# Loading the first x columns and the first weight in halves, and moving three small steps and one weight load in the state-space layer of a two-layer trunk

## The chip, the cores and the metric

The kernel runs on one core of a Trainium2 chip. The metric is the device time of one execution in microseconds (us); the time of a kernel is the median of several runs. One run of each kernel was also recorded by the hardware profiler, and the rows in this document come from that recording. Engines are named as in the profile: PE does the matrix products and the transposes, PEld its weight loads, DVE is the vector engine, ACT the scalar engine, POOL the GpSimd engine, SP the engine that issues most DMAs. Each engine runs its instructions in order; what follows an instruction that waits, waits too.

## The reference

The input x is 1024 frames by 1024 channels in float32. Two layers run one after the other, each adding to x. Cut to what matters:

```python
# layer 0: state-space mixer
h = rmsnorm(x, norm_g[0])
branch, gate = split(h @ s5_w_in[0])            # 1024 x 2048 weight
y = gelu(s5_mixer(branch, ...))                 # 64 groups, 16 channels -> 64 complex states
y = y * sigmoid(y @ s5_w_glu[0] + s5_b_glu[0])
x = x + (y * silu(gate)) @ s5_w_out[0]
# layer 1: gMLP mixer
u, v, gate = split(rmsnorm(x, norm_g[1]) @ sgu_w_in[0])
x = x + (sgu_mixer(gelu(u), gelu(v), ...) * silu(gate)) @ sgu_w_out[0]
return rmsnorm(x, final_g)
```

## The kernel before

Every float32 matrix product is done as three products of "hi" and "lo" parts: hi is the value rounded to the format that PE reads, lo the rest. For the input projection x is transposed by PE (`x_turn`), ACT copies the rounded part into `ahi` (`x_hi`), and DVE writes the difference into `alo` (`x_lo`). A weight panel of 128 columns is loaded into a raw buffer by SP (`w_load`), ACT rounds it into `w_hi` and DVE or POOL subtracts into `w_lo` (`w_split`). There is one raw buffer until a second one is added late; w_load of the next panel waits until the subtraction has read the buffer.

The input projection has 16 output tiles i, each in two halves of 512 frames; a half is 8 steps k of three matmuls with 512 columns. `in_mm` issues the steps and `in_out` (called `evict` later) has DVE multiply the finished PSUM bank by the row factors into the tile `stage`, from where `in_store` writes it to memory. Until all of layer 0's units are done the bank of a half is chosen by a counter modulo the number of banks in the list `banks["mm"]`: four at the beginning, two during the units, four again afterwards. A half can start only when the half that had its bank before is evicted.

At the start the four row blocks of x come in four loads of 512 columns, then weight 0 in one load. PE turns four column blocks, ACT and DVE split them, the weight is split by ACT and POOL, and DVE does some scalar preparation in between (`pull(n)` runs n small instructions of it). While the first three output tiles are computed, the preparation ends, `make_b0(0)` builds the first batch of a small table (three POOL instructions, the tile printed as `b`, from `br`, `bi`, `bn`, `bs`), `phases()` builds the phase table `ph` on POOL, and `tab_ops(0)` builds the first rotation table `e` on POOL.

Then come 19 periods, p from -3 to 15, one for each of 16 units of four groups. A period interleaves, on every engine in the written order, the work of units p, p+1, p+2, p+3 and some steps of the input projection: `mm(n)` takes the next n steps from the list `todo`; when it has taken the last step of a half it appends the half to the list `outs`; `evict()` takes the first entry of `outs`, and does nothing when the list is empty. `FILL0` gives one step at each of the five places of a period with p below 0, `FILL` gives 2, 2, 2, 2, 1 afterwards. `outs` starts with (2, 1) and (3, 0), `todo` with (3, 1), (4, 0), (4, 1) and so on. In period p unit p is rotated (`rot_co` on DVE, `rot_si` on POOL, `rot_add` on DVE, with the table `cs` that SP copies from `e`), scanned (`scan`, the tile `gg`), and rotated back. The first `evict()` of a period stands behind `rot_add` and `scan` on DVE. `k_mm(p+2)` on PE reads the table `b`; batch 1 is built by `make_b0(1)` at the end of period -2.

Unit outputs go to memory (`y_d`) and come back as tiles `lo` through `load_y(k)`: eight DMAs for each k, on SP, the odd ones of k = 7 on ACT. `y_split(k)` splits them on ACT and DVE. Behind period 15 all of load_y(4) to load_y(7) is issued, and then a loop over k takes five steps of the projection, one eviction, one `y_split` and, when a whole tile of the projection is done, a `split` of the weight two tiles on and a `queue` that loads the one after. The last such weight, number 16, is the first panel of the next product (`w_glu`, 384 matmuls).

Up to here `in_order[0]` is true and the order on each engine is the written one. Behind it a planner orders the instructions.

Of the kernel before, what the change touches and what calls it, by code (L numbers as in the profile page):

```python
# [19 lines left out]
F32R = mybir.dt.float32r  # L20
# [6 lines left out]
P = 128  # L27
# [33 lines left out]
def trunk(ctx, tc, x, norm_g, final_g, s5_w_in, A_re, A_im, log_dt, B_re, B_im, C_re, C_im,  # L61
# [211 lines left out]
    def x_hi(half, k):  # L273
        S.activation(ahi[:, k, half * HALF:(half + 1) * HALF], x_ps[half, k], AF.Copy, scale=g0[:, k:k + 1])
# [44 lines left out]

    def in_mm(i, half, ks, between=lambda: None):  # L320
        if ks[0] == 0:
            in_ps[i, half] = mmps()
        hi, lo = in_w[i]
        cs = slice(half * HALF, (half + 1) * HALF)
        ps = in_ps[i, half]
        for k in ks:
            T.matmul(ps, lhsT=hi[:, k], rhs=ahi[:, k, cs], start=k == 0, stop=False)
            T.matmul(ps, lhsT=hi[:, k], rhs=alo[:, k, cs], start=False, stop=False)
        between()
        for k in ks:  # L330
            T.matmul(ps, lhsT=lo[:, k], rhs=ahi[:, k, cs], start=False, stop=k == KT - 1)
# [406 lines left out]
    Q.dma_start(g0, norm_g[0].rearrange("(k p) -> p k", p=P))  # L738
    for b in range(4):
        load_x(0, b, b + 1, 0, HALF)  # L740
    w_load(0)
    load_x(0, 0, 2, HALF, D)
# [44 lines left out]

    for k in range(4):
        x_turn(0, k)
        x_hi(0, k)  # L790
        if k == 2:
            pull(4)
        x_lo(0, k)
        if k == 1:
            w_split(0, GP)
    pull(13)
    in_mm(0, 0, range(0, 4), lambda: x_turns(0, range(4, 8)))
    for k in range(4, 8):
        x_hi(0, k)
        x_lo(0, k)  # L800
    in_mm(0, 0, range(4, 8))
    w_load(2)
# [49 lines left out]
    pull(99)  # L852
    make_b0(0)
    phases()
    c_turn(1)
# [52 lines left out]
    def period(p):  # L908
# [13 lines left out]
        if p == 0:  # L922
            for _ in gen:
                pass
        if here:
            swap_in(p)
            rot_co(p)
            rot_si(p)
# [44 lines left out]
        if p % 2 == 0 and 2 <= p + 4 < 16:  # L973
            put_powers((p + 4) // 2)
            make_b0((p + 4) // 2)

# [8 lines left out]
    for p, ks in ((14, (0,)), (15, (1, 2, 3))):  # L985
        for k in ks:
            load_y(k)
        period(p)
    for k in range(4, 7):
        load_y(k)  # L990
    for i in range(UG):
        out_mm(15, i)
    out_copy(15)
    load_y(7)
    wk_cm.__exit__(None, None, None)
# [5 lines left out]
    for k in range(KT):  # L1001
        mm(5)
        evict()
        y_split(k)
        split(V)
        queue()
# [244 lines left out]
```

## Time and profile before

| | |
|---|---|
| runs, us | 856.35, 854.26, 852.93 |
| median, us | 854.26 |
| profiled execution, us | 857.32 |
| its span, us | 855.2 |
| mean granted clock of PE in it | 0.985 |
| PE busy | 96% of the span |
| DVE, ACT, POOL busy | 60%, 34%, 27% |

The span is from the first to the last instruction of the program; 2.1 us of the profiled execution lie around it. A busy share is an average over stages. In the views, a timeline row is start, length, engine, operation, tiles written and read, shapes, count, and in brackets the engine's idle time before it and what ended that. The clock column of a windows row is the share of full speed that PE was granted: 1.00 is 2.4 GHz, 0.50 is 1.2 GHz.

### The profile page before, as it was taken

Reading aid. Unit: us, or ns where it says so; the run is one execution under the profiler, and the core shown is the slowest. Engines: PE = TensorE matmul, PEld = TensorE weight load, DVE = VectorE, ACT = ScalarE, POOL = GpSimd, SP = SyncE. Lnnn points to the kernel's source line nnn. Section 1 sums busy time; section 2 is a strip of 40 time slices with the busy share of each in tenths; the row PEclk is TensorE's granted clock in tenths of the full one; section 3 lists DMA queues with packets and bytes.
Section 4 is the critical chain, followed back from the end, with each engine's and each line's share of the span. In section 5 each row is a group of like instructions: output and inputs, shape, how many; then the busy total and the mean of one; then the engine's idle time right before and its main releaser. Section 6 shows DMA issues by size and latency. Waiting matters only on the chain.

```text
span 855.2 us, 10992 instructions
## 1 busy us (share of the span) xinstructions
PE 822.1 (96%) x3962; PEld 669.5 (78%) x3962; DVE 511.9 (60%) x1097; ACT 293.8 (34%) x519; POOL 228.9 (27%) x261
## 2 busy tenths in 40 slices
PE   7998899999998999989999999999999899999996
PEld 6776687888886888868888888888888688888884
DVE  8888888888635977863277211211599945452255
ACT  4632444444433765453122322211412122332122
POOL 2059877787520000000000000000057512113221
PEclk9999999999999999989999999999999899999998
DMA  9727787888988623464012321300400012380022
GB/s 278 109 72 185 178 226 197 203 211 203 239 191 190 212 69 111 147 221 125 25 74 82 122 68 49 101 23 1 147 1 1 25 50 77 103 256 9 1 99 98
DMA packets 122678, 102.25 MB, mean 120 GB/s; under 512 B 20480, under 2 KB 103424, under 8 KB 122624
## 3 DMA queue, kind: packets, MB, share of 16 engines
q1 hardware_dynamic: 112144, 94.93, 40.0%
q10 hardware_dynamic: 10480, 6.62, 2.5%
q8 instruction: 31, 0.51, 0.2%
q14 instruction: 23, 0.19, 0.1%
HBM read 67.45 MB, written 25.17 MB: 108 GB/s over the span
## 4 chain that ended last, share of the span: by engine, by line
PE 57%; DVE 18%; DMA 10%; POOL 5%; ACT 4%; issue 3%; SPq 2%; DVEq 0%; POOLq 0%; ACTq 0%
PE mm L74 52%; PE aux L74 5%; DVE c L74 5%; DVE lo L74 4%; DMA lo<-y_d 2%; DMA raw<-in_s_w_in 2%; SPq L74 2%; ACT c L74 2%; POOL w_lo L74 1%; DVE w_lo L74 1%; DMA raw<-in_s_w_out 1%; DVE t L74 1%; POOL e L74 1%; DMA raw<-in_sgu_w_in 1%; POOL et L74 1%
## 5 line engine op out<-in xcount | busy, mean ns | idle before, releaser
L74 PE MATMUL mm<-ahi,w_hi 128*128 128x512 f32 x512 | 210.2, 411 | 3.8 <-DVE stage L74 3.3
L74 PE MATMUL mm<-alo,w_hi 128*128 128x512 f32 x512 | 202.2, 395 | 1.8 <-DVE alo L74 1.8
L74 PE MATMUL mm<-ahi,w_lo 128*128 128x512 f32 x512 | 196.3, 396 | 0.0
L74 PEld LDWEIGHTS mm<-ahi,w_hi 128*128 128x128 f32 x512 | 97.2, 190 | 24.9 <-DVE stage L74 4.1
L74 PEld LDWEIGHTS mm<-alo,w_hi 128*128 128x128 f32 x512 | 97.4, 190 | 21.5 <-DVE alo L74 3.3
L74 PEld LDWEIGHTS mm<-ahi,w_lo 128*128 128x128 f32 x512 | 97.0, 190 | 21.6
L74 DVE TENSOR_TENSOR w_lo<-raw,w_hi 128x1024 fp32r<-128x1024 f32 x28 | 40.4, 1442 | 69.5 <-ACT w_hi L74 69.5
L74 PE MATMUL mm<-c,ahi 128*128 128x512 f32 x256 | 80.3, 396 | 0.0
L74 POOL TENSOR_TENSOR lo<-lo,lnb 128x128 f32<-128x128 f32 x64 | 34.5, 568 | 162.0 <-DVE lo L74 162.0
L74 ACT ACTIVATE w_hi<-raw 128x1024 fp32r<-128x1024 f32 x38 | 40.1, 1056 | 70.0 <-PE mm L74 50.9
L74 POOL TENSOR_SCALAR_AFFINE_SELECT wsn<-wsn 128x1024 f32<-128x1024 f32 x1 | 1.1, 1092 | 231.2 <-DMA wsn<-in_sgu_w_s 231.2
L74 DVE TENSOR_TENSOR c<-mm,c 128x512 f32<-128x512 f32 x32 | 21.9, 691 | 65.3 <-PE mm L74 65.3
L74 PEld LDWEIGHTS mm<-c,ahi 128*128 128x128 f32 x256 | 48.1, 188 | 11.7
L74 PE MATMUL mm<-hi,ahi 128*128 128x512 f32 x128 | 52.0, 407 | 3.0 <-ACT hi L74 2.9
L74 PE MATMUL mm<-hi,w_hi 128*128 128x512 f32 x128 | 51.2, 400 | 2.6 <-ACT w_hi L74 2.6
L74 DVE TENSOR_TENSOR c<-c 128x512 f32<-128x512 f32 x64 | 50.1, 835 | 3.2 <-POOL c L74 3.1
L74 PE MATMUL mm<-hi,alo 128*128 128x512 f32 x128 | 51.9, 407 | 0.0
L74 PE MATMUL mm<-lo,ahi 128*128 128x512 f32 x128 | 51.9, 405 | 0.0
L74 PE MATMUL mm<-lo,w_hi 128*128 128x512 f32 x128 | 51.3, 401 | 0.0
L74 PE MATMUL mm<-hi,w_lo 128*128 128x512 f32 x128 | 51.1, 401 | 0.0
L74 PE MATMUL mm<-ahi,hi 128*128 128x512 f32 x128 | 50.6, 396 | 0.0
L74 PE MATMUL mm<-alo,hi 128*128 128x512 f32 x128 | 50.6, 395 | 0.0
(173 smaller groups left out, 1483.1 us busy)
## 6 DMA issues: line engine op xcount, KB each, us to landing
raw<-in_sgu_w_in SPq DMA_DIRECT2D x24, 512.0 KB, 3.7
cs<-e SPq DMA_DIRECT2D x32, 256.0 KB, 3.9
raw<-in_s_w_in SPq DMA_DIRECT2D x14, 512.0 KB, 5.6
u_d<-stage SPq DMA_DIRECT2D x8, 512.0 KB, 5.3
us<-u_d SPq DMA_DIRECT2D x16, 256.0 KB, 5.1
t_d<-kpad SPq DMA_DIRECT2D x64, 64.0 KB, 3.0
traw<-t_d SPq DMA_DIRECT2D x16, 256.0 KB, 5.3
y_d<-ysb ACTq DMA_DIRECT2D x16, 256.0 KB, 3.2
```

The source lines that it names most:

```text
L74: ins = getattr(self.engine, name)(*args, **kwargs)
```

## The change

Five edits. First, x's first 512 rows come in two loads of 256 columns with half of weight 0 behind each; the weight is split half by half (`w0_split`), `in_mm0` issues the first output half in smaller pieces (the products of `w_lo` apart, so that `in_mm` loses its `between`), and the preparation instructions are pulled 4, 4 and 9 at a time where it was 4 and 13. Second, `make_b0(1)` is issued with `make_b0(0)` ahead of `phases()`, and no longer at the end of period -2. Third, period 0 calls `evict()` once more, ahead of unit 0's rotation. Fourth, behind unit 15 nine steps of the projection, one eviction, the split of weight 15 and the load of weight 16 come ahead of load_y(6) and load_y(7); until then only two banks are in the list. Fifth, the loop over k takes its last steps one turn earlier.

```diff
-    def in_mm(i, half, ks, between=lambda: None):
+    def in_mm(i, half, ks):
...
-        between()
...
-    for b in range(4):
-        load_x(0, b, b + 1, 0, HALF)
-    w_load(0)
+    in_raw[0] = raw_tile([P, KT, P])
+    for q in range(2):
+        load_x(0, 0, 4, q * 256, (q + 1) * 256)
+        Q.dma_start(in_raw[0][:, q * 4:(q + 1) * 4],
+                    s5_w_in[0][q * HALF:(q + 1) * HALF, 0:P].rearrange("(k p) c -> p k c", p=P))
...
-    for k in range(4):
-        x_turn(0, k)
-        x_hi(0, k)
-        if k == 2:
-            pull(4)
-        x_lo(0, k)
-        if k == 1:
-            w_split(0, GP)
-    pull(13)
-    in_mm(0, 0, range(0, 4), lambda: x_turns(0, range(4, 8)))
+    w0 = in_w[0] = [wsp.tile([P, KT, P], F32R, name=f"w_{c}", tag=c) for c in ("hi", "lo")]
+
+    def w0_split(q):
+        ks = slice(q * 4, (q + 1) * 4)
+        S.activation(w0[0][:, ks], in_raw[0][:, ks], AF.Copy)
+        sub_hi(GP, w0[1][:, ks], in_raw[0][:, ks], w0[0][:, ks])
+
+    def in_mm0(ks, part):
+
+        if (0, 0) not in in_ps:
+            in_ps[0, 0] = mmps()
+        for k in ks:
+            for j, src in ((0, ahi), (0, alo)) if part == 0 else ((1, ahi),):
+                T.matmul(in_ps[0, 0], lhsT=w0[j][:, k], rhs=src[:, k, 0:HALF], start=(k, part) == (0, 0) and src is ahi,
+                         stop=(k, part) == (KT - 1, 1))
+
+    for q in range(2):
+        for k in (2 * q, 2 * q + 1):
+            x_turn(0, k)
+            x_hi(0, k)
+            x_lo(0, k)
+        w0_split(q)
+        pull(4)
+        in_mm0((2 * q, 2 * q + 1), 0)
+    pull(9)
+    x_turns(0, range(4, 8))
+    in_mm0(range(0, 4), 1)
     for k in range(4, 8):
         x_hi(0, k)
         x_lo(0, k)
-    in_mm(0, 0, range(4, 8))
+        in_mm0((k,), 0)
+    in_mm0(range(4, 8), 1)
...
     make_b0(0)
+    make_b0(1)
     phases()
...
         if p == 0:
             for _ in gen:
                 pass
+            evict()
         if here:
             swap_in(p)
             rot_co(p)
...
             put_powers((p + 4) // 2)
-            make_b0((p + 4) // 2)
+            if p >= 0:
+                make_b0((p + 4) // 2)
...
-    for k in range(4, 7):
-        load_y(k)
+    load_y(4)
+    load_y(5)
     for i in range(UG):
         out_mm(15, i)
     out_copy(15)
+    mm(9)
+    evict()
+    split(V)
+    queue()
+    load_y(6)
     load_y(7)
...
     banks.update(mm=[0, 1, 2, 3], aux=[4, 5, 6, 7])
     for k in range(KT):
-        mm(5)
-        evict()
+        if k != KT - 1:
+            mm(5)
+            evict()
         y_split(k)
         split(V)
         queue()
```

## Rows read from the trace of the kernel before

**Rows 1.** The page, part 1: busy time, share of the span, number of instructions.

```profile
PE 822.1 (96%) x3962; PEld 669.5 (78%) x3962; DVE 511.9 (60%) x1097; ACT 293.8 (34%) x519; POOL 228.9 (27%) x261
```

**Rows 2.** Waits of PE: who was waited for, us in total, times, longest.

```profile
PE mm L74 <- DVE stage L74: 3.3, 2, 2.8
PE mm L74 <- ACT w_hi L74: 3.0, 2, 2.6
...
PE aux L74 <- POOL b L74: 1.3, 1, 1.3
```

**Rows 3.** Windows: length; busy of PE, PEld, DVE, ACT, POOL; clock, DMA share, GB/s.

```profile
12.05:14.25 2.20, 0.36 (x2) 0.00 (x0) 2.20 (x3) 0.04 (x1) 1.41 (x1) 1.00 1.14 338
...
92.00:95.40 3.40, 3.40 (x12) 2.71 (x11) 3.30 (x6) 1.76 (x3) 3.24 (x6) 0.50 0.45 74
272.80:275.45 2.65, 0.12 (x1) 0.00 (x0) 0.00 (x0) 1.07 (x2) 0.00 (x0) 1.00 1.10 385
276.20:279.60 3.40, 3.40 (x10) 2.38 (x9) 3.40 (x6) 3.24 (x6) 0.00 (x0) 0.52 1.11 357
371.90:378.80 6.90, 6.12 (x14) 4.24 (x15) 4.58 (x7) 4.86 (x8) 0.00 (x0) 0.51 0.66 224
```

**Rows 4.** Timeline of DVE, POOL, PE and ACT at the start, 9 to 20 us.

```profile
9.27 1.41 DVE L74 SCALAR_TENSOR_TENSOR alo<-aux,g,ahi 128x512 fp32r<-128x512 f32 x2
...
11.13 2.41 DVE L74 TENSOR_SCALAR t<-t 128x128 f32<-128x128 f32 x1
...
17.01 2.71 DVE L74 SCALAR_TENSOR_TENSOR alo<-aux,g,ahi 128x512 fp32r<-128x512 f32 x4
...
11.08 2.38 POOL L74 TENSOR_TENSOR w_lo<-raw,w_hi 128x1024 fp32r<-128x1024 f32 x1 [4.28 <-ACT w_hi L74]
...
15.25 1.91 PE L74 MATMUL aux<-ident,xh 128*128 128x128 f32 x16
...
15.89 2.42 ACT L74 ACTIVATE ahi<-aux,g 128x512 fp32r<-128x512 f32 x4 [3.80 <-PE aux L74]
```

**Rows 5.** Timeline: POOL's last of make_b0(0), DVE beside it, POOL's last of make_b0(1).

```profile
54.51 4.38 POOL L74 TENSOR_TENSOR b<-b,b0t 128x128 f32<-128x128 f32 x1
...
54.86 0.70 DVE L74 TENSOR_TENSOR mu<-lp,br 128x512 f32<-128x512 f32 x1
...
82.57 0.45 POOL L74 TENSOR_TENSOR b<-b,b0t 128x128 f32<-128x128 f32 x1
```

**Rows 6.** Timeline of SP and DVE around unit 0's rotation, 81 to 91 us.

```profile
81.80 3.14 SPq L74 DMA_DIRECT2D cs<-e  x4
...
86.34 0.70 DVE L74 TENSOR_TENSOR rot<-rot,cs 128x512 f32<-128x512 f32 x1 [2.60 <-DMA cs<-e]
...
89.75 1.05 DVE L74 TENSOR_TENSOR stage<-mm,rb 128x512 f32<-128x512 f32 x1
```

**Rows 7.** Timeline of DVE: the last eviction ahead of the one in rows 6.

```profile
74.76 1.13 DVE L74 TENSOR_TENSOR stage<-mm,rb 128x512 f32<-128x512 f32 x1
```

**Rows 8.** Timeline behind unit 15; last, the DMA view of a load issued at 72.93.

```profile
244.50 0.48 PE L74 MATMUL mm<-ahi,w_hi 128*128 128x512 f32 x1
...
250.33 0.39 SPq L74 DMA_DIRECT2D raw<-in_s_w_in  x1
...
251.40 18.01 SPq L74 DMA_DIRECT2D lo<-y_d  x28
269.45 0.43 SPq L74 DMA_DIRECT2D raw<-in_s_w_glu  x1
...
249.52 3.67 ACTq L74 DMA_DIRECT2D lo<-y_d  x4
...
256.23 1.06 ACT L74 ACTIVATE w_hi<-raw 128x1024 fp32r<-128x1024 f32 x1 [0.71 <-DMA raw<-in_s_w_in]
...
258.19 1.22 DVE L74 TENSOR_TENSOR w_lo<-raw,w_hi 128x1024 fp32r<-128x1024 f32 x1
...
raw<-in_s_w_in SPq DMA_DIRECT2D x1, 512.0 KB, 4.2
```

## The prediction, made before the changed kernel was run

> **What bounds the kernel now.** I read the page's busy shares first, then the list of what PE waited for, then windows with the granted clock around the longest of those waits, and last the timelines of the engines there. PE is busy for 822.1 us, 96% of the span [rows 1]. So an edit is worth what it takes from PE's idle time or adds to it. All edits act before 283 us. Behind that point 384 matmuls of the next product follow, and they need about 0.23 us each, so what PE gains or loses before is carried to the end. In the part touched, PE's longest waits are 2.8 us for an eviction (the tile stage), 2.6 us for the rounded weight 16 and 1.3 us for the table b [rows 2]. The reader should look at the clock too. After the wait for the weight (PE idle from 272.9 to 275.5) PE runs at 0.52 for 3.4 us, and after the wait for the eviction at 0.50 for 3.4 us: the level of 1.2 GHz instead of 2.4. That costs half of 3.4, 1.7 us, each time. At 12.05 PE stood nearly idle for 2.2 us and the clock stayed at 1.00 [rows 3].
>
> **The start.** The loads become finer, but x is not what comes last there. DVE can't split a column of x before 9.27, because its preparation runs until then, and two columns take it to 10.68. Later DVE stands in one small instruction for 2.41 us, because POOL subtracts the weight at the same time, for 2.38 us. The last four columns start at 17.01, and PE's last products of that half wait for them [rows 4]. So the question is whether DVE comes to 17.01 earlier. In the changed order PE issues the products of columns 0 and 1 first, and the last of these needs the split at 10.68; it is through at 11.0. Only then it turns columns 2 and 3. A column takes 0.5 us to turn (16 column pieces, four to a column, in 1.91 us) and 0.6 us to copy [rows 4], so DVE splits columns 2 and 3, 0.68 each (four in 2.71), from about 12.4 to 13.7. ACT copies the second half of the weight from 12.8 to 13.4, and POOL subtracts it for half of 2.38, 1.2 us, to about 14.7. DVE's 13 small instructions begin at 13.7, stand behind that to 14.7, and need 2.1 us more (in the trace the block ends at 13.5, two column splits take 1.4, and these instructions the rest to 17.0). That gives 16.8 in place of 17.0. The long block is split, but DVE's wait for PE's turns takes what it frees. I take -0.2 us, with bounds of -0.7 (the small instructions get in before POOL's second half) and +0.4 (x's pieces of 1 KB land later than its rows of 2 KB; PE's turn of the second pair then waits). The load of weight 2, which waits for POOL's subtraction, leaves SP 1.2 us later, and those of bn, weight 3 and bs queue behind it on SP. All of x's second half is split and multiplied before the first of their users, and that hides it; without this cover it would cost the 1.2.
>
> **Two batches of beta B ahead.** The three instructions of make_b0(1) end at 83.02 [rows 5], and SP starts to copy the table e at 81.80 [rows 6], when POOL has just finished it: the three cost POOL 1.2 us. Taking them from there removes PE's wait of 1.3 us for b. But they now stand ahead of phases() and of e, which POOL builds one behind the other, so e is done 1.2 us later. The chain goes on from e: SP's copies at 81.80; DVE's rotation at 86.34, which waits for them (2.60 us); then scan and eviction, which ends at 90.8 [rows 6] and lets PE go on. All of that comes 1.2 us later. PE saves 1.3 us on the way and then waits longer for the eviction. I take +1.2 us. PE is idle from about 86.5 to 92.1 then, 5.6 us in place of 2.8. Whether the half level afterwards lasts 3.4 us or 6.9, as at 371.9 [rows 3], I can't tell: bounds 0 (the new instructions find a gap on POOL) and +2.9.
>
> **One more eviction in period 0.** It does nothing. With one step at each of five places, periods -3 to -1 take 15 steps of todo: all eight of (3, 1) and seven of (4, 0). The evictions of (2, 1), (3, 0) and (3, 1) have been issued, the last at 74.76 [rows 7], and the next one in the trace is that at 89.75. The eighth step of (4, 0) is issued in the first mm of period 0, behind the new call. So outs is empty there, and the call returns. Cost 0, and the wait of 2.8 us stays.
>
> **Weight 16 ahead of the last y loads.** SP issues 28 pieces of y in 18.01 us and only then, at 269.45, the load of weight 16, for which PE waits [rows 8]. In the new order 12 of them come behind it, 12 x 0.64 = 7.7 us, so it leaves at about 262 and lands near 268 (5.8 us, as weight 15 took), before PE needs it. That takes away 2.6 us of waiting and the 1.7 us of the half level, 4.3 us. The last y pieces are late by one issue at most, and are needed only at the seventh and eighth step of the next product.
>
> What is late next is a bank. Nine steps now run while the list has two banks. The counter gives (13, 1) bank 1 (27 modulo 2) where it gave bank 3, and (14, 1), number 29, takes bank 1 of four. So (14, 1) waits for the eviction of (13, 1). On DVE that now stands behind the subtraction of weight 15, which stands behind ACT's rounding, which waits for the landing of weight 15. PE's 123 matmuls from 244.50 to 272.8 are 0.230 us apart, so it comes to (14, 1), 51 matmuls in, at 256.2. Weight 15 is issued at 250.33. In the trace it lands at about 256.1 (ACT starts at 256.23), 5.8 us later; a load of the same size on a quiet queue took 4.2 us [rows 8], that is 254.5. Four pieces of y that ACT issues at 249.52 are in its way now and will come behind it, so I take 255.2. From there on 0.1 + 1.06 for the rounding, 1.2 for the subtraction and 0.7 for the eviction with its hand-over: PE goes on 3.1 us after the landing, at 258.3. The new wait is 2.1 us (bounds 1.4 and 3.0; 0 if the weight lands far earlier than any such load did). The wait of 2.2 us at 12.05 left the clock alone, those of 2.6 and 2.8 did not; I take no half level here. Together -4.3 + 2.1 = -2.2 us, bounds -4.3 and +0.4 (3.0 with a half level).
>
> Sum: -0.2 + 1.2 + 0 - 2.2 = -1.2 us. The profiled execution took 857.32 us (span 855.2), so it would take 856.1. It lies 3.1 us above the median of the runs, 854.26; taken from that, 853.1 us.
>
> **The rivals.** (1) Weight 15 lands so early that (14, 1) hardly waits: -0.2 + 1.2 - 4.3 = -3.3, 851.0 us. For it speaks that the queue is freer; against it, that no such load took under 4.2 us. Chance 0.13. (2) The new wait takes 3.0 us and brings the half level again: -0.2 + 1.2 + 0.4 = +1.4, 855.7 us. That is today's landing unchanged. Chance 0.14. (3) POOL's new instructions cost the chain nothing. The last one of make_b0(0) took 4.38 us where its like takes 0.45, while DVE ran products of SBUF tiles of 0.70 us, one behind the other [rows 5]; if the new ones could slip into that run, phases() would begin as today, and the sum is -1.2 - 1.2 = -2.4, 851.9 us. The row speaks against it, since the first one didn't slip in. The Trainium skill (SBUF — State Buffer, Who interferes with whom) says that the two engines share a port pair, and that the one that comes second waits until the first one's instruction has ended; by that, POOL would get in after one DVE instruction of 0.7 us, which is the time of this rival. The row shows a wait through several such instructions, so I hold to the row. Chance 0.05. (4) The wait for the eviction at unit 0 goes away, as the call's place suggests: -0.2 - 1.3 - 2.8 - 1.7 - 2.2 = -8.2, 846.1 us. The count of steps excludes it unless the lists run otherwise than I read them. Chance 0.03. (5) Slower: ACT stands still at its four issues of y. They come behind the rounding of weight 15 now and ahead of every y_split, and took 3.67 us in the trace [rows 8], part of it waiting. If each waits for pieces of y that SP issues late, ACT's splits start late. DVE's chain behind them has 16 pieces of 0.68, a weight of 1.2 and an eviction, about 13 us, and PE wants the last piece at 272.8 + 2.1 + 21 x 0.23 = 279.7. So from 266.7 on each us that ACT stands longer costs PE one. If ACT stood until 272.7, about 3 us behind SP's last issue of y, that is 6.0: -1.2 + 6.0 = +4.8, 859.1 us. For it speaks that the issues have moved behind others; against it, that SP is still at the fifth tile of y when ACT comes to them. Chance 0.07.
>
> **How the numbers follow.** My forecast has 0.55. The rest, 0.03, is the planner, which orders everything behind the first layer's units and may order it otherwise. The measurement can tell about 0.5%, 4.3 us, from no change. The range takes in rivals 1 to 3: down to -0.7 + 1.2 - 4.3 = -3.8, 850.5 us, and up to +0.4 + 1.8 + 0.4 = +2.6, 856.9 us (1.8: the chain's 1.2 and a third of the longer half level's 1.7). Faster by more than 0.5% are rival 4 and the lower tails of the forecast, of rival 1 and of the planner, 0.12; slower by more, most of rival 5 and the upper tails of rival 2 (a longer half level) and of the planner, 0.11; the rest, 0.77, lies within.
>
> **What would show it.** In the changed kernel's profile: DVE's last four splits at the start still begin near 17; PE's wait for b is gone; SP's first copies of cs start 1.2 us later against DVE's preparation, and PE's wait for stage at unit 0 has grown to about 5 us; no eviction stands ahead of unit 0's rotation; a new wait for stage of about 2 us at 256; none for w_hi at 273. I am wrong if the start gains over 1 us, if PE doesn't wait at 256, or if an eviction appears ahead of the rotation.

## The result, and the profile of the changed kernel

| | before | changed |
|---|---|---|
| median, us (10 runs each) | 854.59 | 860.97 |
| lowest and highest, us | 852.57 to 857.16 | 856.81 to 862.11 |
| profiled execution, us (span) | 857.32 (855.2) | 862.11 (860.4) |

The ratio is 1.007, with a 95% interval of 1.0056 to 1.0083: the changed kernel is slower by 6.0 us (4.8 to 7.1). The prediction was 853.1 us with a range up to 856.9, so it was wrong, and in direction too. Of its three terms that aren't zero, one held in the profiles (+1.2 for beta B) and two fell (-0.2 for the start, -2.2 for the tail).

Busy time, the line that answers to [rows 1]: PE is busy 2.6 us longer for the same 3962 instructions; its mean granted clock was 0.979 where it was 0.985.

```profile
PE 824.7 (96%) x3962; PEld 670.7 (78%) x3962; DVE 511.7 (59%) x1097; ACT 293.7 (34%) x520; POOL 228.8 (27%) x262
```

Waits of PE (us in total, times, longest), against [rows 2]: the wait for b is gone, that for the tile stage has grown from 2.8 to 5.5, and a wait of 2.0 for lo, the split of y, is new. What is left for w_hi is a wait at the start.

```profile
PE mm L74 <- DVE stage L74: 6.6, 3, 5.5
...
PE mm L74 <- DVE lo L74: 2.0, 1, 2.0
...
PE mm L74 <- ACT w_hi L74: 1.3, 1, 1.3
```

Windows of the changed kernel (columns as in [rows 3]), each inside a stretch at a granted clock of 0.50: at the start (the stretch lasts from 8.5 to 15.4 us), behind unit 0's eviction (6.8 us, from 93.9 to 100.7, where it was 3.4), and behind the wait for lo (3.4 us, from 288.4 to 291.8).

```profile
9.50:15.30 5.80, 4.50 (x18) 3.61 (x17) 4.50 (x15) 2.09 (x4) 1.28 (x1) 0.50 1.09 354
94.00:100.30 6.30, 4.79 (x13) 3.88 (x14) 5.63 (x10) 3.72 (x8) 5.52 (x7) 0.50 0.34 63
288.60:291.00 2.40, 2.40 (x7) 1.92 (x6) 2.40 (x4) 2.40 (x4) 0.00 (x0) 0.50 0.41 164
```

At the start this column can't be compared with before. Before shows 1.00 there, but its trace has no record of the clock ahead of 10.1 us. Its first turns began 0.21 us apart up to 10.0 us, twice the 0.11 us of the 16 at 15.25 [rows 4]: the spacing of the lower level. So by the spacing that level ended at 10 us in before and at 15.4 in the changed kernel. The turns in before:

```profile
7.15 3.37 PE L74 MATMUL aux<-ident,xh 128*128 128x128 f32 x16
```

DVE at the start, against [rows 4]: it waits 3.46 us for log_dt and then is late by 1.7 us at the first split of x and by 3.4 at the last four (20.40 against 17.01). In between it waits 1.70 for the turns of columns 2 and 3.

```profile
5.47 0.66 DVE L74 TENSOR_SCALAR t<-t 128x64 f32<-128x64 f32 x3 [3.46 <-DMA t<-in_s_log_dt]
...
10.94 1.41 DVE L74 SCALAR_TENSOR_TENSOR alo<-aux,g,ahi 128x512 fp32r<-128x512 f32 x2
12.27 1.38 DVE L74 SCALAR_TENSOR_TENSOR t<-t,t 128x128 f32<-128x128 f32 x1
...
15.82 1.41 DVE L74 SCALAR_TENSOR_TENSOR alo<-aux,g,ahi 128x512 fp32r<-128x512 f32 x2 [1.70 <-ACT ahi L74]
...
20.40 2.71 DVE L74 SCALAR_TENSOR_TENSOR alo<-aux,g,ahi 128x512 fp32r<-128x512 f32 x4
```

That log_dt and A_im land late stands in the DMA view (queue, KB, and us from issue to landing). First the kernel before, then the changed one; both issue the three small loads at 0.81, 1.30 and 1.95 to 1.96.

```profile
t<-in_s_log_dt ACTq DMA_DIRECT2D x1, 32.0 KB, 3.3
...
t<-in_s_A_im ACTq DMA_DIRECT2D x1, 16.0 KB, 4.6
```

```profile
raw<-in_s_w_in SPq DMA_DIRECT2D x1, 256.0 KB, 6.1
t<-in_s_log_dt ACTq DMA_DIRECT2D x1, 32.0 KB, 4.6
...
t<-in_s_A_im ACTq DMA_DIRECT2D x1, 16.0 KB, 6.3
```

Around unit 0, against [rows 6]: DVE's rotation at 91.17, behind a wait of 4.15 us for cs, then the eviction, then PE. No eviction stands ahead of the rotation: the extra call did nothing.

```profile
91.17 0.70 DVE L74 TENSOR_TENSOR rot<-rot,cs 128x512 f32<-128x512 f32 x1 [4.15 <-DMA cs<-e]
...
94.40 1.05 DVE L74 TENSOR_TENSOR stage<-mm,rb 128x512 f32<-128x512 f32 x1
...
95.50 0.79 PE L74 MATMUL mm<-ahi,w_hi 128*128 128x512 f32 x1 [5.55 <-DVE stage L74]
```

In the tail, against [rows 8]: the wait for the bank at 262 is there, 0.76 us. Then come two stands of DVE that I had not foreseen: 4.05 us until the store of tile 13 has been done, and 1.80 us at a product of the next block (the tile c) that waits for its load. The eviction of (15,1) and the last two y splits stand behind that, and PE waits for them.

```profile
262.19 0.50 PE L74 MATMUL mm<-ahi,w_hi 128*128 128x512 f32 x1 [0.76 <-DVE stage L74]
...
278.83 0.69 DVE L74 TENSOR_TENSOR stage<-mm,rb 128x512 f32<-128x512 f32 x1 [4.05 <-DMA z_d<-stage]
279.44 2.49 DVE L74 TENSOR_TENSOR lo<-lo,hi 128x512 fp32r<-128x512 f32 x4
283.73 2.97 DVE L74 TENSOR_TENSOR c<-c 128x512 f32<-128x512 f32 x3 [1.80 <-DMA c<-z_d]
286.61 0.69 DVE L74 TENSOR_TENSOR stage<-mm,rb 128x512 f32<-128x512 f32 x1
287.21 2.49 DVE L74 TENSOR_TENSOR lo<-lo,hi 128x512 fp32r<-128x512 f32 x4
...
287.95 0.50 PE L74 MATMUL mm<-lo,w_hi 128*128 128x512 f32 x1 [2.01 <-DVE lo L74]
```

Where the time came from is best seen by matching PE's instructions one by one: how much later the same matmul starts than in the first profile of before (medians over 4 us). All rows but the first are runs told in the next section.

| us later at | 60 | 92 | 142 | 262 | 290 | 390 |
|---|---|---|---|---|---|---|
| changed | +3.4 | +5.6 | +4.7 | +6.0 | +5.3 | +5.1 |
| before, second profile | +1.6 | +1.6 | +1.7 | +2.7 | +0.4 | +1.3 |
| before, third profile | -0.8 | -1.0 | -0.8 | 0.0 | -2.8 | -2.3 |
| first edit alone | +3.6 | +5.0 | +4.2 | +4.6 | +0.6 | +1.5 |
| second edit alone | +0.4 | +2.6 | +1.8 | +1.8 | -2.2 | -0.2 |
| tail alone | +0.1 | -0.1 | 0.0 | +1.6 | -2.2 | -1.2 |
| working eviction | +0.5 | -3.4 | +1.2 | +1.8 | -2.3 | -1.7 |
| mended tail | +0.5 | +1.2 | +0.4 | +0.4 | -3.7 | +0.4 |

The first profile of before has its longest wait in this part, for weight 16, between 262 and 290; a kernel without that wait gains some 4 us on it there, so the last two columns flatter every kernel. The column at 60 shows what the start is worth, and it follows DVE: the last four splits of the first half start 3.4 us later in the changed kernel, 1.7 with the order alone (below), and 0.8 earlier in the third profile of before, and PE at 60 is +3.4, +1.7 and -0.8.

### The profile page after: what moved, and what is told of

The parts are those of the page before. It is cut to its first block, busy times and chain, and to the rows that moved or that the text cites. A ratio compares the mean times of both kernels' runs of the same rounds, so it can differ in the third digit from the quotient of the medians.

```text
span 860.4 us, 10979 instructions
## 1 busy us (share of the span) xinstructions
PE 824.7 (96%) x3962; PEld 670.7 (78%) x3962; DVE 511.7 (59%) x1097; ACT 293.7 (34%) x520; POOL 228.8 (27%) x262
## 4 chain that ended last, share of the span: by engine, by line
PE 53%; DVE 18%; DMA 9%; POOL 7%; ACT 4%; SPq 4%; issue 3%; DVEq 0%; POOLq 0%; ACTq 0%
PE mm L74 48%; DVE c L74 5%; PE aux L74 4%; SPq L74 4%; DVE lo L74 4%; DMA raw<-in_s_w_in 2%; ACT c L74 2%; DVE w_lo L74 2%; DMA cs<-e 1%; POOL ph L74 1%; DMA lo<-y_d 1%; POOL et L74 1%; POOL hh L74 1%; POOL e L74 1%; DMA raw<-in_sgu_w_in 1%
## 5 line engine op out<-in xcount | busy, mean ns | idle before, releaser
L74 ACT ACTIVATE w_hi<-raw 128x1024 fp32r<-128x1024 f32 (+1 forms) x39 | 40.3, 1033 | 71.4 <-PE mm L74 51.0
```

What stands on the lines that cost most here:

```text
L74: ins = getattr(self.engine, name)(*args, **kwargs)
```

## The experiments

The times are summed up here; each ratio is to runs of the kernel before on the same chip. The ratio is not that of the two medians, so the last column, worked out from it, can differ from their difference. An interval is some 3 us wide, so that a difference of 1 us between two kernels is not settled by times alone; the profiles say where it arises. Three executions were taken for a profile alone: the kernel before twice more (857.07 and 853.79 us) and the loads by row pairs (858.36).

| kernel | median (before) | ratio, 95% interval | in us |
|---|---|---|---|
| first edit alone | 858.35 (855.07) | 1.0029, 1.0012 to 1.0046 | +2.5 |
| - its loads alone | 855.00 (855.07) | 1.0001, 0.9983 to 1.0019 | +0.1 |
| - its order alone | 856.24 (854.63) | 1.0017, 1.0001 to 1.0034 | +1.5 |
| - with the small loads ahead | 854.13 (854.15) | 1.0008, 0.999 to 1.0025 | +0.7 |
| second edit alone | 855.67 (855.07) | 1.0005, 0.999 to 1.0019 | +0.4 |
| tail alone | 856.59 (855.07) | 1.0017, 1.0003 to 1.003 | +1.5 |
| - store ahead | 856.51 (854.63) | 1.0013, 0.9994 to 1.0032 | +1.1 |
| - and four banks | 856.03 (854.63) | 1.0006, 0.9989 to 1.0024 | +0.5 |
| - and the last eviction behind the splits | 854.93 (854.84) | 0.9996, 0.998 to 1.0012 | -0.3 |
| change without the first edit | 857.05 (854.47) | 1.0026, 1.001 to 1.0042 | +2.2 |
| change with the mended tail | 856.26 (854.84) | 1.0016, 1.0001 to 1.0031 | +1.4 |
| working eviction | 855.22 (854.47) | 1.0013, 0.9992 to 1.0033 | +1.1 |
| mended tail, weight 0 on DVE | 853.46 (854.84) | 0.9992, 0.9973 to 1.001 | -0.7 |
| the same and the working eviction | 854.75 (854.84) | 0.9993, 0.9975 to 1.0011 | -0.6 |
| the same and the small loads ahead | 854.27 (854.15) | 1.0009, 0.9995 to 1.0023 | +0.8 |

### Each edit alone

Three kernels carry the first, the second, and the fourth with the fifth edit of the diff above, and nothing else.

> The first edit alone (x and weight 0 in halves, with the new order of the first half's products). Theory S: the profile of the changed kernel showed PE 3.4 us later than before from 18 us on, with DVE's first split at 10.94 instead of 9.27 and the last four at 20.40 instead of 17.01; if the edit does that, the time is 3.4 us over that of the kernel before, and these two splits stand at the late places again. Rival: the small loads of log_dt and A landed late in that one recording by chance; then the first split is back near 9.3, the last four near 16.8, and the time is that of before within 0.5 us.

Measured +2.5 us. The late splits stand again at 11.00 and 20.66, so it was not that one recording alone; a later profile of the same start has them at 9.45 and 18.31 (the change with the mended tail, below), so it is not every execution either. What follows: of the three parts the start costs the most by itself, though its interval overlaps that of the tail.

> The second edit alone (make_b0(1) ahead of phases()). Theory: PE's wait for b (1.3 us) is gone, its wait for stage at unit 0 is about 5.5 us instead of 2.8, and the half clock behind it lasts about 6 us instead of 3.4: +1.2 to +1.8 us. Rival: POOL finds room for the three instructions beside DVE; then the wait for stage stays near 2.8 us, and the time falls by 1.2 us.

Measured +0.4. The wait for b is gone, the wait for stage is 5.54, and PE runs at half clock behind it, as in the changed kernel. The edit does what was said, +2.2 at 92 us against its own start and +2.4 at 103; but 1.0 of that is back at 142, because the waits of 0.41 and 0.48 us for xn and stage that the first profile of before has at 136 and 137 are gone. These two in before:

```profile
135.98 0.43 PE L74 MATMUL aux<-xn,b 128*32 128x128 f32 x8 [0.41 <-DVE xn L74]
136.88 0.51 PE L74 MATMUL mm<-ahi,w_hi 128*128 128x512 f32 x1 [0.48 <-DVE stage L74]
```

> The fourth and fifth edits alone (weight 16 ahead of load_y(6) and load_y(7)). Theory T: the wait for weight 16 goes (-4.3 us), a wait of about 1 us for a bank comes at 256, and DVE stands about 4 us at the first eviction of tile 15, because its stage buffer is free only when the store of tile 13, which SP issues behind load_y(6) and load_y(7), has been done; PE then waits about 2 us for the last split of y and runs at half clock behind it. Sum 0 to +0.5 us against before. Rival, as predicted: no such stand, -2.2 us (-4.3 for weight 16, +2.1 for the bank).

Measured +1.5. All three waits of theory T are there: the bank 0.95, DVE's stand for the store 4.26, PE's wait for lo 0.42. PE doesn't wait for weight 16, but no gain is left in the times. The profile can't show all of that: its execution took 854.41 us, 2.2 under this kernel's median. The missing gain asks what this wait costs in a usual execution of the kernel before.

### The kernel before, twice more

No edit.

> The kernel before once more, for a second profile of it. Theory P: the first profile (857.32 us, about 2.5 us above the median) showed a wait of 2.7 us for weight 16 and 3.4 us of half clock behind it that a usual execution doesn't have in full; in this profile PE's product with weight 16 then starts 1 us or more earlier against PE's work ahead of it, without the half clock, and an execution near the median reaches 350 us about 2 us earlier. Rival: the wait and the half clock are there in every execution (2.5 us or more, and 3.4 us), and the 2.5 us come from somewhere behind 350 us.

> The kernel before a third time. The same two theories: a wait of under 2.5 us for weight 16 without half clock behind it in an execution near the median (theory P), or both in full in each execution (rival).

Theory P holds in its main point. The waits for weight 16 are 1.46 and 0.89 us by the row (2.57 in the first profile; the expectations count from one matmul's start to the next, 0.15 more), and the clock stays at 1.00 behind both. PE's row and then the window behind it, first in the second profile:

```profile
277.20 0.50 PE L74 MATMUL mm<-hi,w_hi 128*128 128x512 f32 x1 [1.46 <-ACT w_hi L74]
```

```profile
277.20:280.60 3.40, 3.39 (x13) 2.44 (x14) 3.40 (x5) 3.38 (x7) 0.00 (x0) 1.00 1.08 351
```

And in the third:

```profile
273.99 0.50 PE L74 MATMUL mm<-hi,w_hi 128*128 128x512 f32 x1 [0.89 <-ACT w_hi L74]
```

```profile
274.00:277.40 3.40, 3.39 (x13) 2.45 (x14) 3.40 (x5) 3.09 (x7) 0.00 (x0) 1.00 1.11 329
```

Of the ten profiles with the old tail (three of before, seven of experiments) four show the wait, 2.57, 1.46, 0.89 and 0.51 us, and only the first has the half clock. So the 4.3 us that I priced were the extreme of ten; 0.9 to 1.5 is what the other two profiles of before offer. The second profile took 857.07 us, which is no time near the median; there the expectation of an early 350 us doesn't fit, since its start is 1.6 us late. That is not DVE's first split, which stands at 9.23; the granted clock is 0.50 from 9 to 18 us there. At weight 16 both other profiles gain on the first: 2.3 and 2.8 us between 262 and 290 (table).

This wait also takes up lateness. PE came to weight 16 later by 4.6 us with the first edit and by 1.8 with the second (table, at 262), and in both it did not wait at all.

### The start: loads or order

Loads alone, with the order of before:

```diff
-    for b in range(4):
-        load_x(0, b, b + 1, 0, HALF)
-    w_load(0)
+    in_raw[0] = raw_tile([P, KT, P])
+    for q in range(2):
+        load_x(0, 0, 4, q * 256, (q + 1) * 256)
+        Q.dma_start(in_raw[0][:, q * 4:(q + 1) * 4], ...)
```

> Of the first edit only the loads (x in column halves, weight 0 in halves), with the compute order of before. Theory L: the four bigger and finer loads at the head of SP's queue make ACT's loads of log_dt and A land 1 to 2 us later; DVE's first split is then near 10.9 and the time 1.5 to 3.4 us over before. Rival O: the order of the products costs it (PE's products of two columns stand ahead of the turns of the next two), and the loads alone cost under 0.5 us, with the first split near 9.3.

The first split is at 11.01, and PE is 3.1 us late at 60 us; yet the time is +0.1 (-1.5 to +1.6). The last four splits start 2.0 us late, at 18.98; the rest goes with a granted clock of 0.50 from 16.8 to 20.2 us, while PE turns the last four columns. By the same matching PE is +3.2 at 262 and -1.1 at 290: there is no wait for weight 16 and no half clock, and against the first profile of before the lateness is taken up. That doesn't explain the median, since this execution took 857.09 us, 2.1 above it. Theory L is right on the delay in this execution and wrong on the time; whether a usual one has the delay isn't known.

Order alone (`w0_split` and `in_mm0`, with the loads of before):

> Of the first edit only the new order of the products (weight split in halves, smaller pieces of the first output half), with the loads of before. Theory: with log_dt back near 4.1 DVE's first split stands near 9.3; as predicted the last four stand near 16.8, PE is between 0.7 us earlier and 0.4 later from 20 us on, and the time is within 1 us of before. Rival: the order itself costs, by PE standing at half clock while it multiplies columns 0 and 1 ahead of the next turns; then the last four splits come near 18.5 or later, and the time is 1.5 to 3.3 us over before.

The rival holds: the splits of columns 2 and 3 are at 14.13 where I predicted 12.4, the last four at 18.74 where I predicted 16.8. PE's products of columns 0 and 1 begin only when ACT has rounded the half of the weight, and then run 0.43 us apart instead of 0.23; the turns of columns 2 and 3 stand behind them at 12.32, and DVE waits 1.70 us.

```profile
9.78 0.62 ACT L74 ACTIVATE w_hi<-raw 128x512 fp32r<-128x512 f32 x1
...
10.45 0.79 PE L74 MATMUL mm<-ahi,w_hi 128*128 128x512 f32 x1 [1.29 <-ACT w_hi L74]
11.04 0.63 PE L74 MATMUL mm<-alo,w_hi 128*128 128x512 f32 x1
...
12.32 1.72 PE L74 MATMUL aux<-ident,xh 128*128 128x128 f32 x8
...
14.13 1.42 DVE L74 SCALAR_TENSOR_TENSOR alo<-aux,g,ahi 128x512 fp32r<-128x512 f32 x2 [1.70 <-ACT ahi L74]
...
18.74 2.71 DVE L74 SCALAR_TENSOR_TENSOR alo<-aux,g,ahi 128x512 fp32r<-128x512 f32 x4
```

What makes the small loads late? Two loads of two row blocks each:

```diff
-    for b in range(4):
-        load_x(0, b, b + 1, 0, HALF)
+    for b in (0, 2):
+        load_x(0, b, b + 2, 0, HALF)
```

> The kernel before with x's first half in two loads of two row blocks each, 512 columns wide: 512 KB per load as in the halves by columns, but in pieces of 2 KB as before. It tells what delays the small loads. Theory F: the number of pieces in the loads behind them does (512 of 1 KB or 512 B in each halved load, 128 of 2 KB in one of before); with 256 pieces log_dt lands at 4.1 to 4.7, not at 5.5. Rival: the bytes of a load do; then log_dt lands near 5.5 here too.

Both in part: log_dt lands at 4.2 (pieces of 2 KB), but A_im at 8.1, as late as behind the halves. The first split is at 10.84. So A is late behind a load of 512 KB in this shape too. For log_dt the pieces can't be the whole cause: with the row loads of before it landed at 4.1 to 4.2 in twelve profiles and at 5.2 in a thirteenth (the working eviction below), and with halved loads at 5.4 to 5.5 in three and at 4.2 in the fourth.

A look at the times of issue explains A. In the profiles of before, of the halved loads and of the row pairs ACT issues A_im 0.02 to 0.03 us behind SP's second load, and A_im lands 0.2 us behind that load (before: 6.5 behind 6.3; changed: 8.2 behind 8.1). In one profile with halved loads, the change with the mended tail below, ACT was 0.02 us ahead (1.93 against 1.95), and A_im landed at 6.4, ahead of it (7.2); in one with the loads of before likewise (1.93 against 1.94), and A_im landed at 5.3. The Trainium skill (DMA: Bandwidth & Descriptors, Queues, rings and completion order) says that a completion increment lands only after every earlier write of that DMA engine, across its queues. The landings of A_im agree, 0.2 us behind the load ahead of it; that of log_dt, issued ahead of all of them, isn't explained by it. The order of issue can be fixed:

```diff
-    S.dma_start(anat[:, 0], A_re[0])
-    S.dma_start(anat[:, 2], A_im[0])
+    S.dma_start(g0, ...)
...
-    Q.dma_start(g0, ...)
+    Q.dma_start(anat[:, 2], A_im[0])
+    Q.dma_start(anat[:, 0], A_re[0])
```

> The first edit alone, but SP issues A_im and A_re ahead of its loads of x, and ACT issues log_dt and g. Theory: SP's and ACT's loads are served one behind another in the order of issue, so a small load that is issued behind a halved load waits for all of its pieces; with A ahead, A_re and A_im land before 5.5 (6.7 and 8.2 in the first edit alone), DVE's first split starts near 9.4 or, if x is last then, near 10, and the time is 1 to 2 us under the first edit alone (858.35), 1 to 2 over before, which is the cost of the new order. Rival: the small loads are slowed by the traffic of the pieces, whatever the order; then log_dt still lands near 5.5 and the first split stays at 11.

The small loads land at 3.7 to 4.4, all of them, and DVE's first split is at 8.90. The last four are at 18.10, late by the order alone. The time is +0.7 (-0.9 to +2.1) where the first edit alone had +2.5 (1.0 to 3.9). The intervals overlap, but the profiles agree with it: the last four splits are 1.1 us late and PE at 60 is +1.1, where the first edit alone has +3.6 twice. DMA view:

```profile
t<-in_s_log_dt ACTq DMA_DIRECT2D x1, 32.0 KB, 2.9
t<-in_s_A_im SPq DMA_DIRECT2D x1, 16.0 KB, 3.1
```

### Together: the change without its first edit

> All of the change but its first edit. Theory S: the halved loads at the start cost the most; with them undone 2 to 3 us of the 6 stay, as the second edit alone (+0.6) and the tail alone (+1.5) add up to. Rival: the edits only hurt together, because the tail's new order takes the wait that absorbs a delay away; then this kernel, with the second edit's delay and the new tail, is 4 us or more over before.

Measured +2.2 (0.9 to 3.6): theory S. The parts alone add up to 2.5 + 0.4 + 1.5 = 4.4, the change has 6.0. The missing 1.6 are about what the wait for weight 16 takes up where the old tail stands; by the intervals this isn't shown.

### An eviction that really stands ahead

```diff
         if p == 0:
             for _ in gen:
                 pass
+            mm(n[0])
+            evict()
...
-        mm(n[0])
+        if p != 0:
+            mm(n[0])
```

> The kernel before with an eviction that really stands ahead of unit 0's rotation: in period 0 the first two steps of the projection, and then one eviction, are issued ahead of the rotation (PE's order stays as it was). Theory C: the changed kernel's extra call found an empty list; here it finds half (4,0), DVE evicts it near 83.8, in the 2.6 us in which it waits for cs, PE's wait of 2.8 us for stage at 88 goes with the half clock behind it, 4 us in all at that point; by the end -2 to -4 us, less what the wait for weight 16 takes back. Rival: PE's next wait in unit 0 (for the rotation, or for the next bank) takes its place, and the time is within 1 us of before.

The eviction is there (DVE, 85.02) and PE's wait of 2.8 us is gone. But the time is +1.1 (-0.7 to +2.8): the rival. PE, 3.4 us ahead at 92, waits for DVE in one unit after the other, and at 142 nothing is left. PE's longer waits up to 140; the kernel before has only the two at 136 and 137 behind its eviction:

```profile
92.92 0.43 PE L74 MATMUL aux<-xn,b 128*32 128x128 f32 x8 [1.65 <-DVE kpad L74]
...
105.11 0.43 PE L74 MATMUL aux<-xn,b 128*32 128x128 f32 x8 [1.39 <-DVE xn L74]
115.77 0.42 PE L74 MATMUL aux<-xn,b 128*32 128x128 f32 x8 [0.68 <-DVE xn L74]
126.57 0.42 PE L74 MATMUL aux<-xn,b 128*32 128x128 f32 x8 [0.82 <-DVE xn L74]
137.22 0.43 PE L74 MATMUL aux<-xn,b 128*32 128x128 f32 x8 [0.68 <-DVE xn L74]
```

So DVE sets the pace of the first units, though PE looks busy there. What delays DVE at the start goes through; what PE alone wins does not. Matching DVE's instructions in the same way shows it in all twenty profiles: however early or late PE is at 92, at 142 it is, within 0.2 us, where DVE was at 86. (In the profile of the working eviction DVE is late by itself, because log_dt landed at 5.2 there and the first split stands at 10.33.)

| us later | changed | second edit alone | change without the first edit | working eviction | weight 0 on DVE and the working eviction | before, third profile |
|---|---|---|---|---|---|---|
| DVE at 86 | +4.7 | +1.7 | +2.3 | +1.3 | -1.1 | -0.8 |
| PE at 92 | +5.6 | +2.6 | +3.0 | -3.4 | -4.4 | -1.0 |
| PE at 142 | +4.7 | +1.8 | +2.3 | +1.2 | -1.2 | -0.8 |

### Mending the tail

First the store of tile 13 ahead of load_y(6), then four banks as well:

```diff
     out_copy(15)
+    banks.update(mm=[0, 1, 2, 3], aux=[4, 5, 6, 7])
     mm(9)
     evict()
     split(V)
     queue()
+    evict()
+    queue()
     load_y(6)
```

> The fourth and fifth edits, with the eviction of (13,1) and the store of tile 13 issued ahead of load_y(6). Theory T: in the tail alone DVE stood 4.26 us at the eviction of (15,0), until the store of tile 13, queued behind load_y(6) and load_y(7), had been done; with the store ahead of them it doesn't, the last splits of y come 3 us or more earlier, and PE's wait for them (0.6 to 2.2 us) is gone. The wait for the bank near 256 (0.9 to 1.9 us) stays. So 0.6 to 2 us less than the tail alone (856.6 against 855.1). Rival: the splits of y are late because y lands late, and PE waits for them as long as before.

> As the kernel with the store ahead, and the list of four banks is set ahead of the nine steps instead of behind them. Theory: the new wait for a bank near 256 goes as well, since (13,1) and (14,1) then have banks of their own; what is left is the gain of weight 16, whose wait was 2.7, 1.6 and 1.05 us in three profiles of before: 1 to 3 us under before. Rival: a wait for a bank that the last unit's outputs hold, or for y, takes its place; then it is within 0.5 us of the kernel with the store ahead.

The waits named are gone (store 0, bank 0 with four banks), but neither time, +1.1 and +0.5, is clear of the tail alone or of before. With both mended PE waits 5.40 us for lo. DVE, free at 272, stands 8.13 us at a product of the next block that the planner put ahead of the eviction of (15,1) and the last splits; its data come with a load of z that SP issues behind all of y.

```profile
280.28 3.28 DVE L74 TENSOR_TENSOR c<-c 128x512 f32<-128x512 f32 x4 [8.13 <-DMA c<-z_d]
283.47 0.68 DVE L74 TENSOR_TENSOR stage<-mm,rb 128x512 f32<-128x512 f32 x1
284.07 2.49 DVE L74 TENSOR_TENSOR lo<-lo,hi 128x512 fp32r<-128x512 f32 x4
...
284.81 0.80 PE L74 MATMUL mm<-lo,w_hi 128*128 128x512 f32 x1 [5.40 <-DVE lo L74]
```

The fifth edit makes room for that: it takes the last steps one turn earlier, so that (15,1) is evicted ahead of y_split(6) and y_split(7), and DVE must wait for PE there. Putting the eviction behind them:

```diff
         if k != KT - 1:
             mm(5)
-            evict()
+            if k != KT - 2:
+                evict()
```

> The kernel with four banks and the store ahead, and the eviction of (15,1) behind the last split of y instead of ahead of the last two. Theory: the cost of the tail is the written order of the fifth edit: (15,1) is evicted ahead of y_split(6) and y_split(7), DVE has to wait for PE there, the planner fills that wait with products of the next block, and these stand until z_d has been loaded (1.5 to 8.1 us). With the eviction behind them DVE splits y as it lands, the last split ends near 276.5, PE has no wait between 255 and 290, and the time is 1 to 3 us under that with four banks alone (856.0), 1 to 2 under before. Rival: the planner still puts the next block's products ahead of a split; then PE still waits for lo near 284.

> The full change with that tail. Theory: the tail's 1.5 us and its new waits go, the start's and the second edit's cost stays, and since no wait for weight 16 absorbs it now, it is seen in full: 1.5 to 3 us under the changed kernel (861.0), 3 to 4.5 us over before. Rival: the tail's waits come from the lateness that the start brings; then it stays within 1 us of the changed kernel.

The theory holds for the mechanism: DVE splits the last y at 275.44 and waits for c only behind that, and PE has no wait for a bank, for weight 16 or for lo. In the full change the new tail brings 861.0 to 856.3 us (ratio 1.0016 against 1.007). Alone it doesn't beat the kernel before (-0.3, -1.7 to +1.0): PE is 3.7 us ahead at 290 and at 390 is back at +0.4. On the way it waits three times for the lo parts of the next weights, which DVE makes too late, 1.6 us in all by the rows; by the matching each of the three places costs about 1.05 us (from -3.7 at 330 to -0.5 at 360). The first profile of before has no such wait up to 369, the second and the third have one each (0.50 and 0.45). The last 1.0 us is lost between 366 and 380, where PE waits for the next panel in every profile (0.6 to 2.9 us); I haven't followed what sets that.

```profile
275.44 1.29 DVE L74 TENSOR_TENSOR lo<-lo,hi 128x512 fp32r<-128x512 f32 x2 [0.43 <-ACT hi L74]
280.44 2.42 DVE L74 TENSOR_TENSOR c<-c 128x512 f32<-128x512 f32 x2 [3.71 <-DMA c<-z_d]
...
330.97 0.50 PE L74 MATMUL mm<-hi,w_lo 128*128 128x512 f32 x1 [0.53 <-DVE w_lo L74]
343.23 0.51 PE L74 MATMUL mm<-hi,w_lo 128*128 128x512 f32 x1 [0.53 <-DVE w_lo L74]
355.49 0.50 PE L74 MATMUL mm<-hi,w_lo 128*128 128x512 f32 x1 [0.52 <-DVE w_lo L74]
```

### A shorter chain on DVE

With the mended tail; first weight 0 subtracted by DVE, then the working eviction, then the small loads ahead of x as well:

```diff
         if k == 2:
             pull(4)
+            sub_hi(V, w0[1], in_raw[0], w0[0])
```

> The kernel with the mended tail, and weight 0 subtracted by DVE behind the first four small instructions, not by POOL beside them (PE's order is that of before). Theory: DVE's stand of 2.2 us beside POOL goes and 1.2 us of its own work comes: its last four splits of the first half start at 16.0 to 16.7 instead of 17.0, and PE from 20 us on is 0.3 to 1 us earlier, to the end: 0.3 to 1 us under the kernel with the mended tail. Rival: DVE has to wait there for ACT's rounding of weight 0 (11.1 us), and nothing is gained.

> The last one with the eviction of (4,0) that really stands ahead of unit 0's rotation. Theory: between 90 and 140 us the units on DVE set the pace, so the 2.8 to 3.5 us that PE wins at 88 are waited away again for xn by 140, and the time is within 0.7 us of the kernel without it. Rival: with an earlier DVE the gain stays, and it is 1.5 us or more under.

> The kernel with the mended tail, the working eviction and weight 0 subtracted by DVE, and the small loads ahead of x. Theory: in the kernel before A lands at 6.2 to 6.5 and DVE's preparation ends at 9.3; x's row blocks land up to 7.7, half a us later here. So DVE's first split moves by 0.3 us at most, and the time is that of the kernel without this (854.75, and 853.46 without the eviction) within 1 us. Rival: A was what came last; then DVE is 0.5 us or more earlier and the time 1 us or more under.

DVE's stand of 2.41 us [rows 4] is gone, its own subtraction costs 1.22, and the last four splits start at 16.20. The third profile of before has them at 16.23 without any edit, so this gain is within what one kernel shows from run to run. The times are -0.7, -0.6 and +0.8 us, each interval takes in 0, and so none is shown to beat the kernel before. In the last one x became what DVE waits for (1.18 us, first split at 10.23): x is issued 0.77 us later than in before, not half a us, its last row block lands at 8.95 against 7.67, and DVE's preparation doesn't cover that.

```profile
11.52 1.22 DVE L74 TENSOR_TENSOR w_lo<-raw,w_hi 128x1024 fp32r<-128x1024 f32 x1
...
16.20 2.72 DVE L74 SCALAR_TENSOR_TENSOR alo<-aux,g,ahi 128x512 fp32r<-128x512 f32 x4
```

## Why the prediction was wrong

**What bounds the kernel.** "What PE gains or loses before is carried to the end" is the step that failed first. Three places take up what PE alone wins or loses: the units up to 140 us, where DVE sets the pace (3.4 us won, none left), the wait for weight 16 (up to 2.6 us), and the next product (with the mended tail 4.1 us won were lost again between 290 and 390, about 3 of them at waits for DVE's weights). I took 96% busy for a bound at each place. A loss was carried there: the changed kernel is +5.3 at 290 and +5.1 at 390.

**The start (predicted -0.2, the first edit alone +2.5).** Two steps failed. "DVE can't split a column of x before 9.27, because its preparation runs until then" took the preparation as fixed; it begins with log_dt and needs A, and both landed 1.2 to 1.7 us later. For A_im the cause is the bigger load issued just ahead of it; for log_dt it stays open. I had asked only when x lands. And "it is through at 11.0" put PE's products right behind the split; they had to wait for the half weight until 10.45, ran at 0.43 us apart, and ended at 12.3. The sum for the moved chain was 16.8; by order alone it was 18.7. My bound of +0.4 came from x's pieces only, and the sum used the full clock, where PE ran at the spacing of the lower level until about 13.7 us. Right was the reading that DVE, not x, is what the last products wait for.

**Beta B (predicted +1.2, alone +0.4, in the profiles +1.3 and +1.4 at 142, against PE's own lateness at 60).** Each step came as described: no wait for b, cs later (SP's first copy at 83.51 in the second edit alone, against 81.80), PE's wait 5.5, and the longer half level that I put in the bound. What stays at 142 is DVE's lateness at 86, which is 1.3 to 1.4 us more than PE's at 60 in three of the four profiles with this edit (0.5 in the fourth; -0.3 to +1.1 in the sixteen without it). What PE alone loses beyond that goes into the slack of 0.9 us at 136, the term that the sum left out. Rival 3 fell, and with it what it drew from the Trainium skill (SBUF — State Buffer, Who interferes with whom), that POOL would get in after one DVE instruction of 0.7 us: the new POOL instructions did not slip in; in the second edit alone the last one of make_b0(0) again took 4.36 us, and the new three came behind it.

**The extra eviction (predicted 0).** Right; the count of steps in the lists gave it. Rival 4's mechanism exists when the call is put right, but its price of 2.8 + 1.7 us was waited away by 142.

**The tail (predicted -2.2, alone +1.5).** The new wait for the bank came as worked out, at 262, and took 0.76 to 1.69 us in four profiles where 2.1 was forecast. Two terms were wrong. The gain of 4.3 us was read from the one profile, which lay 2.7 us above the median of ten runs; I noted that difference and moved the sum by it, but didn't ask which wait it might be. It was in the main this one: 0.9 and 1.5 us without half clock in the next two, which gain 2.8 and 2.3 us there. And "the last y pieces are late by one issue at most" looked only at SP. On DVE stood the store of tile 13, queued behind the y loads (4.05 us), and the eviction of (15,1), which the fifth edit moves ahead of the last two splits, with the planner's product in front of it. I gave the planner 0.03 and no price; rival 5 had the right place, the end of DVE's chain of splits, with the wrong cause: ACT's issues of y took 3.4 us, as before, and PE's wait doesn't go back to them.

**What stays open.** Why the tail costs 4.7 us in the full change (861.0 against 856.3) and about 1.7 alone (856.6 against 854.9) isn't settled. In the profiles the difference sits at PE's wait for lo: with the half clock behind it, it costs 3.6 us between 282 and 290 in the changed kernel (+1.7 to +5.3), 1.6 in the change without the first edit and 0.5 in the tail alone, and these two have no half clock there. Why the wait is longer in the full change I can't say. The profile of the change with the mended tail also had the lucky order of A_im and an early log_dt (4.2), and the share of that among its runs isn't known. Of the twelve runs of the first edit alone three took 853.7 to 855.8 us and the others 857.7 to 859.8, which such a share would explain, but no profile of the three was taken.

## What to carry to other kernels

Before a wait is priced, look at it in more than one profile, above all when the profiled execution lies above the median: the wait that makes the edit attractive may be what made that execution long. Follow a move to every queue it passes, up to who waits for a store or a buffer there, and read on each engine which written step now has to wait, because a planner may fill that place with something worse. When a load is made bigger or is issued earlier, list the small loads that are issued around it and who starts with them.

## What the hardware showed

- A small load of 16 KB lands with its neighbours: 0.02 us ahead of or behind a load of 256 KB in the order of issue made 6.4 or 8.2 us of its landing. log_dt, issued ahead of all of them, landed at 4.1 to 4.2 in twelve of thirteen profiles with row loads behind it (5.2 in the other) and at 5.4 to 5.5 in three of four with halved ones (4.2 in the other); what makes it late isn't explained by these runs.
- Matmuls ran 0.43 us apart from 10.45 to 12.3 in the kernel with the order alone, the spacing of 1.2 GHz, while the window's granted clock is shown as 1.00. The first record of the clock in that trace begins at 13.7 us; ahead of the first record the column shows 1.00 whatever the spacing.
- The same program's PE was 1.6 us later or 0.8 us earlier at 60 us, in two more profiles, and kept that up to 142 (+1.7, -0.8).
